# Differential-attention scores as fp32 products of 32 rows, four maps in four row quarters of the array, two heads at a time

## The chip, the cores and the metric

The kernel runs on one core of a Trainium2 chip. The metric is device time in microseconds of one execution, the median of several runs. The engines are TensorE (PE; its weight loads are listed as PEld), VectorE (DVE), ScalarE (ACT), GpSimd (POOL) and the DMA queues, which SyncE (SP), GpSimd and others issue to.

## The reference, cut to what matters

The program is a two-part transformer on 512 tokens of width 1024: a first block (mixing by two attentions, attention over a memory, a mixture of experts), then further layers. The change lies in the first step, differential attention with 8 heads, each with two maps of 32 features, and 64 value features:

```python
q1, q2 = q[..., :32], q[..., 32:]
k1, k2 = k[..., :32], k[..., 32:]
...
def attn_map(qb, kk):
    sc = jnp.einsum('bhqd,bhkd->bhqk', qb, kk, preferred_element_type=jnp.float32) * scale + bias
    return jax.nn.softmax(jnp.where(mask, sc, NEG_INF), axis=-1)
a = attn_map(qb1, k1) - lam * attn_map(qb2, k2)
o = jnp.einsum('bhqk,bhkd->bhqd', a.astype(v.dtype), v, preferred_element_type=jnp.float32)
o = o * lax.rsqrt(jnp.mean(o * o, axis=-1, keepdims=True) + RMS_EPS) * gain
```

The mask is causal and the bias is minus a head's slope times the distance of the positions, so a query block of 128 tokens needs 128, 256, 384 or 512 keys. A second attention (latent attention, 8 heads) follows, both results go through one output projection, and the residual is added.

## The kernel before

Activations are feature-major, `[128, 512]` per chunk. Large products are made of fp32r parts: an operand is split into a high part (ScalarE, L406 or L409) and a low part (VectorE, L407 or L410), and three products (L399, L400, L401, 24 of them to a block of 128 output features) replace one of fp32. Weights stream from DRAM through rings of buffers on SP's queue and are split in the same way.

The mixing stage (`mix`, L1719) works through the list `MSEQ` in this order, each letter a step: `p` queries and keys of a pair of heads, `v` values, `h` a head of differential attention, `r` the rotary table, `c`, `k`, `n` the projections and norms of latent attention, `m` keys and values of the memory. The list sets priorities; the tile framework orders the instructions of each engine when the program is built, so that steps interleave, and it sets the semaphores. An engine executes its own instructions in that order.

- `pair(c)` (L1756) makes queries and keys of heads 2c and 2c + 1. It evacuates a block's product times 1/rms (L1749, L1751) into a tile of the ring `sq` (three buffers), splits it into two more tiles of the same ring (L406, L407), writes the parts to DRAM, three times 32 rows for each map (L1766, tile `qkd`), and reads them back (L1771, tile `qk`) so that a map's 96 rows stand under each other. DMAs of this step are issued by GpSimd.
- `attend(h)` (L1857) then needs one fp32r product with 96 rows for a map's scores of a query block (L1872, tile `sc`, two banks). VectorE adds the distances and takes the minimum (L1874, L1878), ScalarE makes the exponentials and their sums (L1880), VectorE joins the two maps (L1884 to L1886). `av` transposes the result on TensorE (L2018, two banks), ScalarE copies it (L2020), and L2010 multiplies it with the values (`po`, two banks). At a head's end come square, sum, power on GpSimd (L1894) and scaling (L1895); after two heads the result is transposed (L1900) and split.

Latent attention uses the same six banks afterwards; its scores (L1969) are fp32 products with 128 rows. Elsewhere in the program, L728 and L1327 are fp32 scores with 64 rows; L1327 takes its two heads from rows 0 to 63 and 64 to 127 in turn. L1353 multiplies with the values, a head in each half of the array's columns. Two more banks (`pmm`) serve the projections everywhere.

Of the kernel before, what the change touches and what calls it, by code (L numbers as in the profile page):

```python
# [6 lines left out]
F32 = mybir.dt.float32  # L7
# [6 lines left out]
P = 128  # L14
# [13 lines left out]
MSEQ="v0 p1 h0 r0 v1 h1 p2 h2 c0 h3 c1 p3 h4 h5 k1 k0 n0 m0 h6 m1 h7 m2"  # L28
PQ=(0,4)
NB0=3  # L30
QP=6
# [13 lines left out]
SB3=7  # L45
# [12 lines left out]
# ---------------------------------------------------------------- host layout  # L58
# [50 lines left out]
def constants():  # L109
    """Arrays that depend on shapes alone, by the part that uses them."""  # L110
# [39 lines left out]
    # blocks of 8, and the blocks under and over the diagonal that a doubling joins  # L150
# [24 lines left out]
def pack(inp):  # L175
# [38 lines left out]
    # a piece holds the same input features for both experts of a pair  # L214
# [13 lines left out]
    # heads that share a block of features  # L228
# [47 lines left out]
# ---------------------------------------------------------------- kernel  # L276

class K:
    def __init__(self, tc, d, sm_off, phases=None, dbg=None):
        self.tc, self.nc, self.d = tc, tc.nc, d  # L280
        self.sm_off = sm_off
        self.dbg = dbg or {}
        self.phases = phases
        self.cst_off = {n: (ph,) + v for ph, c in constants().items() for n, v in c.off.items()}
        self.cst_t = {}
        self.nblk, self.gates = 3, []
        # pieces that the program starts with
        self.early = []
        self.lo_eng = None
# [4 lines left out]
    # -- small helpers  # L294
# [19 lines left out]
    def room(self, st, *, raw, parts):  # L314
        """Room for streamed weights: raw tiles, and tiles of each part; more of it until st closes."""
# [12 lines left out]
    def all_raw(self, st):  # L328
        """The room for parts is for raw tiles too, until st closes."""
# [9 lines left out]
    def experts(self):  # L339
        """The experts' weights in the order of their use."""  # L340
# [8 lines left out]
    def ahead(self):  # L349
        """Load one more piece of the experts' weights, behind the last load."""  # L350
# [7 lines left out]
    def piece(self, kind, dt):  # L358
        """The next tile of streamed weights, from the rings by turns."""
# [4 lines left out]
    def fetch(self, ap, kper):  # L364
        """Start the load of one streamed piece of kper chunks, in tiles of whole chunks."""
# [12 lines left out]
    def parts(self, raw):  # L378
        """A piece split into its two parts; the result gives both for chunk c, columns a to b."""
# [16 lines left out]
    def mm3(self, ps, a, b, first, last):  # L396
        """ps += (a0 + a1)^T (b0 + b1), without the product of the two low parts."""
# [14 lines left out]
    def rpow(self, out, sums, scale, tag="rp"):  # L412
        """out = (sums * scale + EPS) ** -0.5"""
# [6 lines left out]
    def stats(self, chunks, dim, tmp, ntok=T, bank=None, both=False):  # L420
        """Feature-major chunks -> 1/rms per token: token-major [P, nt] and broadcast [P, ntok]."""
# [24 lines left out]
    def rows_of(self, bc, rt, ps):  # L446
        """Token-major columns as rows that every partition has."""
# [7 lines left out]
    def two_norms(self, g1, g2, bank, pool):  # L455
        """Products' operand and factors for rms_norm(rms_norm(x) * g1) * g2; the first 1/rms as rows."""
# [5 lines left out]
        # sums of x^2 and of the squares of the first norm's results, side by side  # L462
# [26 lines left out]
    def norm_split(self, gname, pool=()):  # L489
        """Split x * gain into two parts; 1/rms is left for the products' results. GpSimd takes the chunks in pool."""  # L490
# [9 lines left out]
    def start(self, gname, both=False):  # L500
        """Split x * gain, and 1/rms."""
# [49 lines left out]
    def out_proj(self, src, hs):  # L551
        """x += W^T h."""
# [25 lines left out]
            # brings the functions' table in  # L578
# [44 lines left out]
    def last_norm(self, gname):  # L623
        """The result, rms_norm(x), by halves of the tokens."""
# [60 lines left out]
    def mem_keys(self, m, wk, n, dst):  # L685
        """Keys feature-major [P, n / 128, 256], kept in DRAM."""
# [9 lines left out]
    def mem_values(self, m, wv, n, dst):  # L696
        """Values [P, 2, n], kept in DRAM."""
# [7 lines left out]
    def mem_kv(self, src, pool, n):  # L705
        """Keys and values back on the chip."""
# [5 lines left out]
    def mem_attn(self, q, kv, dh, mh, ml, wk, ps_s, ps_t, ps_o, part=range(4)):  # L712
        """q: feature-major chunks times -1/sqrt(dh); mh, ml: [P, chunks, T] for the result."""
# [72 lines left out]
    # -- swiglu  # L786
    def ffn(self, l, mid=None, end=None):
        tc, nc, d = self.tc, self.nc, self.d
        hs, rt, bc = self.start(f"ln_ffn_2{l}")
        with ExitStack() as st:  # L790
# [6 lines left out]
            for half in range(2):  # L797
# [24 lines left out]
                # the very last by halves of the tokens, for the norm to start on  # L822
# [17 lines left out]
    def gdn(self):  # L840
        tc, nc, d = self.tc, self.nc, self.d
        with ExitStack() as st:
            e = lambda **k: st.enter_context(tc.tile_pool(**k))
            gp = e(name="gdp", bufs=1)
            # the first block's last norm and this one's in one; the residual waits in DRAM, its room is needed
# [22 lines left out]
            # gates  # L868
# [18 lines left out]
            def gates():  # L887
# [4 lines left out]
                # the other halves of what comes as 2 silu  # L892
# [29 lines left out]
                # gc as rows, exactly in three parts: a product spreads the sum of a head's over all partitions  # L922
# [29 lines left out]
            def silu2(y, t):  # L952
                """y = 2 silu(y); tanh is in the same table as exp."""
# [35 lines left out]
                # both come as 2 silu: 4 EPS  # L989
# [20 lines left out]
                # decays: column gc minus row gc  # L1010
# [12 lines left out]
                # its diagonal blocks of 8  # L1023
# [24 lines left out]
            def invert(h, A, Dg):  # L1048
                """Transposes of the inverses of a head's unit triangular matrices, by doubling the blocks.

                Chunks go by twos: of the second the transpose is inverted, so that at every doubling the two
                fill different rows and one product serves both. Chunks lie in the order 0, 2, 1, 3."""
                # heads by turns have their own room, so that two can be under way
# [9 lines left out]
                # blocks of 8 first, every row of an inverse on its lane, with its block's coefficients beside it  # L1063
# [29 lines left out]
                for lv in range(3, 7):  # L1093
# [4 lines left out]
                    def pick(t, odd):  # L1098
                        """Of every two blocks one of the first chunks, and the other of the second chunks."""
# [152 lines left out]
    def swa(self):  # L1252
# [3 lines left out]
        with ExitStack() as st:  # L1256
# [23 lines left out]
            # keys and values, with the gain on the weights  # L1280
# [27 lines left out]
            def attend(c, q):  # L1308
                """Heads c and c + 6."""
# [4 lines left out]
                for n0 in range(0, 4, 2):  # L1314
# [32 lines left out]
                    # a head in each half of the array's columns  # L1347
# [44 lines left out]
    # -- experts  # L1392
    def moe(self):
        tc, nc, d = self.tc, self.nc, self.d
        with ExitStack() as st:
# [13 lines left out]
            with ExitStack() as s2:  # L1409
# [3 lines left out]
                # 1/rms is left for the slots  # L1413
# [3 lines left out]
                # tokens on partitions  # L1417
# [31 lines left out]
                def first_max(p, n, pref, name):  # L1449
                    """One-hot of the first place of the maximum, and the maximum."""  # L1450
# [601 lines left out]
```

## Time and profile before

| | us |
|---|---|
| median of 3 runs | 2067.1 |
| lowest, highest | 2065.58, 2067.19 |
| span of the profiled execution | 2066.2 |
| TensorE busy in the span | 1970.3 |
| VectorE, ScalarE, GpSimd busy | 1041.0, 741.3, 378.4 |

The profile is of one execution, and its span runs from the first to the last instruction of the program; the median lies 0.9 us above it. Busy times are sums over the whole program, whose stages have different limits; matmuls are pipelined, so that a busy TensorE is not TensorE at its peak. The mixing stage takes roughly the first 300 us, and its differential attention the time up to about 222 us.

### The profile page before, as it was taken

What the parts mean: (1) busy time and instruction counts of PE and PEld (TensorE: products, weight loads), DVE (VectorE), ACT (ScalarE), POOL (GpSimd) and SP (SyncE); (2) the same over time, 40 slices, a digit from 0 to 9 for tenths busy, and PEclk for the clock granted to TensorE, in tenths of its full rate; (3) what the DMA queues carried; (4) which work ended last, traced back from release to release, by engine and by line L of the source; (5) the groups of instructions that cost most, each with busy time, mean ns of one, the idle gap of its engine ahead of it and who ended that gap; (6) DMA issues with size and microseconds to landing.
All of it is one profiled execution on the core that took longest, in us unless ns stands there. A gap on an engine that the chain in (4) does not pass through costs nothing.

```text
span 2066.2 us, 26427 instructions
## 1 busy us (share of the span) xinstructions
PE 1970.3 (95%) x10030; PEld 1520.2 (74%) x10030; DVE 1041.0 (50%) x2139; ACT 741.3 (36%) x1465; POOL 378.4 (18%) x364
## 2 busy tenths in 40 slices
PE   8689999989999999999999999999999999999997
PEld 6569668784555558778877788888876688888887
DVE  6368755661322236788855543343436654433434
ACT  4357653631111124344453332222325642222221
POOL 3223134110000001445412110011111021101111
PEclk9889999999999999999999999999999999999999
DMA  6754125149988962211112232332321033233322
GB/s 203 173 130 123 47 62 178 39 164 353 338 293 302 340 231 95 61 42 52 52 57 91 86 90 85 112 93 82 101 92 35 18 102 96 83 98 112 94 82 70
DMA packets 91458, 256.07 MB, mean 124 GB/s; under 512 B 18680, under 2 KB 21824, under 8 KB 91328
## 3 DMA queue, kind: packets, MB, share of 16 engines
q1 hardware_dynamic: 73520, 240.34, 35.0%
q0 software_dynamic: 16144, 12.66, 3.2%
q8 instruction: 81, 1.33, 0.3%
q10 hardware_dynamic: 1664, 1.34, 0.2%
q14 instruction: 49, 0.40, 0.1%
HBM read 241.65 MB, written 12.58 MB: 123 GB/s over the span
## 4 chain that ended last, share of the span: by engine, by line
PE 70%; DVE 4%; DMA 2%; ACT 1%; POOL 1%; issue 1%; DVEq 0%; ACTq 0%
PE mmp L399 16%; PE mmp L400 15%; PE mmp L401 15%; PE pgu L1548 6%; PE py L1548 3%; PE psx L1614 3%; PE pgt L1564 3%; DMA raw<-in_w_swa_dram 1%; PE sc L1327 1%; PE po L748 1%; DVE lo L407 1%; PE tp L961 1%; PE po L1353 1%; PE pt L1339 0%; DVE cv L949 0%
## 5 line engine op out<-in xcount | busy, mean ns | idle before, releaser
L399 PE MATMUL mmp<-xh,hi 128*128 128x512 f32 (+1 forms) x1328 | 523.4, 394 | 1.4 <-ACT xh L406 0.7
L400 PE MATMUL mmp<-xl,hi 128*128 128x512 f32 (+1 forms) x1328 | 517.5, 390 | 0.9 <-DVE xl L410 0.9
L401 PE MATMUL mmp<-xh,lo 128*128 128x512 f32 (+1 forms) x1328 | 517.0, 389 | 0.0
L406 ACT ACTIVATE hi<-raw 128x1024 fp32r<-128x1024 f32 (+2 forms) x256 | 252.4, 987 | 645.7 <-PE mmp L400 557.2
L407 DVE TENSOR_TENSOR lo<-raw,hi 128x1024 fp32r<-128x1024 f32 (+1 forms) x242 | 280.4, 1160 | 140.2 <-ACT hi L406 137.1
L399 PEld LDWEIGHTS mmp<-xh,hi 128*128 128x128 f32 x1328 | 253.3, 191 | 54.3 <-issue 3.0
L400 PEld LDWEIGHTS mmp<-xl,hi 128*128 128x128 f32 x1328 | 253.1, 191 | 50.5 <-issue 1.4
L401 PEld LDWEIGHTS mmp<-xh,lo 128*128 128x128 f32 x1328 | 252.8, 190 | 50.2 <-issue 0.7
L807 POOL TENSOR_TENSOR g<-g,rbc 128x512 f32<-128x512 f32 x44 | 75.5, 1716 | 509.0 <-ACT g L806 509.0
L400 PE MATMUL mmp<-alo,hi 128*128 128x512 f32 (+1 forms) x374 | 141.9, 380 | 0.0
L399 PE MATMUL mmp<-ahi,hi 128*128 128x512 f32 (+1 forms) x374 | 141.9, 380 | 0.0
L401 PE MATMUL mmp<-ahi,lo 128*128 128x512 f32 (+1 forms) x374 | 141.9, 379 | 0.0
L433 POOL TENSOR_TENSOR sqt<-sqt 128x512 f32<-128x512 f32 (+1 forms) x50 | 69.4, 1389 | 241.6 <-ACT sqt L429 223.7
L809 DVE TENSOR_TENSOR a<-mmp,g 128x512 f32<-128x512 f32 x44 | 30.4, 691 | 145.0 <-PE mmp L401 145.0
L805 DVE TENSOR_TENSOR g<-mmp,rbc 128x512 f32<-128x512 f32 x44 | 30.4, 691 | 112.5 <-PE mmp L401 112.5
L399 PEld LDWEIGHTS mmp<-ahi,hi 128*128 128x128 f32 x374 | 70.4, 188 | 14.1
L401 PEld LDWEIGHTS mmp<-ahi,lo 128*128 128x128 f32 x374 | 70.4, 188 | 14.1
L400 PEld LDWEIGHTS mmp<-alo,hi 128*128 128x128 f32 x374 | 70.4, 188 | 14.0
L1564 PEld LDWEIGHTS pgt<-G,tok 128*128 128x128 f32 x512 | 61.6, 188 | 10.9 <-issue 8.9
L943 POOL MEMSET pad<- 128x4 f32 x18 | 1.7, 102 | 368.3 <-DVE xl L410 346.8
L1564 PE MATMUL pgt<-G,tok 128*128 128x256 f32 x512 | 64.6, 282 | 1.0 <-ACT xl L1566 1.0
L1615 DVE TENSOR_TENSOR x<-psx,x 128x512 f32<-128x512 f32 x64 | 43.3, 687 | 43.2 <-PE psx L1614 42.3
(517 smaller groups left out, 3121.8 us busy)
## 6 DMA issues: line engine op xcount, KB each, us to landing
raw<-in_w_egu_dram SPq DMA_DIRECT2D x128, 512.0 KB, 7.9
raw<-in_w_gu_dram SPq DMA_DIRECT2D x88, 512.0 KB, 3.5
raw<-in_w_ed_dram SPq DMA_DIRECT2D x64, 512.0 KB, 8.1
raw<-in_w_out_dram SPq DMA_DIRECT2D x24, 512.0 KB, 3.6
raw<-in_w_gdn_dram SPq DMA_DIRECT2D x24, 512.0 KB, 3.6
raw<-in_w_dn_dram SPq DMA_DIRECT2D x32, 384.0 KB, 3.1
raw<-in_w_dn_dram SPq DMA_DIRECT2D x32, 320.0 KB, 2.8
raw<-in_w_qk_dram SPq DMA_DIRECT2D x12, 512.0 KB, 7.9
```

What stands on the lines that cost most here:

```text
L399: mm(ps, a[0], b[0], start=first, stop=False)
L400: mm(ps, a[0], b[1], start=False, stop=False)
L401: mm(ps, a[1], b[0], start=False, stop=last)
L406: nc.scalar.activation(hi, src, AF.Copy)
L407: (eng or nc.vector).tensor_tensor(lo, src, hi.bitcast(F32), OP.subtract)
L433: (nc.vector if i == len(chunks) - 1 else nc.gpsimd).tensor_tensor(acc, acc, s, OP.add)
L805: nc.vector.tensor_tensor(g, pg, bc, OP.mult)
L807: nc.gpsimd.tensor_tensor(g, g, bc, OP.mult)
L1548: nc.tensor.matmul(ps[hb], a[:, hb], w[b][:, o:o + 512], start=first, stop=last)
L1564: nc.tensor.matmul(pgt[:, 256 * j:256 * j + 256], toks[k][:, t, cs], G[:, t], start=k + t == 0, stop=k + t == 4)
L1614: nc.tensor.matmul(psx, ys[k][:, a, c * P:(c + 1) * P], ss[a], start=a + k == 0, stop=a + k == 2)
L1615: nc.vector.tensor_tensor(self.x[c], psx, self.x[c], OP.add)
```

## The change

Queries and keys of a pair of heads stay in two fp32 tiles of 128 rows: 32 rows for each of the four maps. `attend` takes a pair of heads, and a map's scores are one fp32 product of 32 rows at partition 0, 32, 64 or 96, each into a bank of its own. Splits, DRAM tile and DMAs of `pair` go. Differential attention gets a ring of five banks for scores and transposes and one bank for the output of a pair (both heads' steps at a pair's end are done at once); latent attention opens its own banks afterwards. The order list has four pairs in place of eight heads. Several rings change their size or place (queries and keys 4 tiles, softmax tiles 9 instead of 7, the split latent activations 3 tiles of their own), and comments are removed.

```diff
-MSEQ="v0 p1 h0 r0 v1 h1 p2 h2 c0 h3 c1 p3 h4 h5 k1 k0 n0 m0 h6 m1 h7 m2"
+MSEQ="v0 p1 v1 h0 r0 p2 c0 h1 c1 p3 h2 k1 k0 n0 m0 h3 m1 m2"
-QP=6
+QP=4
-SB3=7
+SB3=9
...
-            dp = e(name="mixd", bufs=2, space=bass.MemoryType.DRAM)
+            cq_p = e(name="mixc", bufs=3)
-            ps_s = e(name="ps_s", bufs=2, space=PSUM)
-            ps_t = e(name="ps_t", bufs=2, space=PSUM)
-            ps_o = e(name="ps_o", bufs=2, space=PSUM)
+            ps_d = dst.enter_context(tc.tile_pool(name="ps_d", bufs=5, space=PSUM))
+            ps_o = dst.enter_context(tc.tile_pool(name="ps_od", bufs=1, space=PSUM))
...
-                t = B("qk")
+                t = qp.tile([P, T], F32, name="qk", tag="qk")
...
             def pair(c):
-                dr = dp.tile([2, 4, 96, T], F32R, name="qkd", tag="qkd")
-                for x, slots in ((0, (0, 0, 1)), (1, (0, 1, 0))):
-                    t = qk(c + 4 * x)
-                    two = [self.sq.tile([P, T], F32R, name="qks", tag="sq") for k in range(2)]
-                    self.split(*two, t)
-                    for i, k in enumerate(slots):
-                        nc.gpsimd.dma_start(dr[x, :, 32 * i:32 * i + 32], two[k])
-                out = []
-                for a in range(2):
-                    out.append([D("qk")[:96] for x in range(2)])
-                    for x in range(2):
-                        nc.gpsimd.dma_start(out[a][x], dr[x, 2 * a:2 * a + 2].rearrange("m p t -> p m t"))
-                return out
+                return qk(c), qk(c + 4)
...
-            def attend(h):
+            def attend(c):
+                q, k = pairs[c]
+                slopes = [2.0 ** -(2 * c + a + 1) for a in range(2)]
+                po = ps_o.tile([P, 4, 2, 64], F32, name="po", tag="po")
...
                 for i in range(4):
                     n = (i + 1) * P
+                    sc = [ps_d.tile([P, T], F32, name="sc", tag="s")[:, :n] for m in range(4)]
+                    for m in range(4):
+                        r = slice(32 * m, 32 * m + 32)
+                        nc.tensor.matmul(sc[m], q[r, i * P:n], k[r, :n], start=True, stop=True)
                     es = []
-                    for m in range(2):
-                        ps = ps_s.tile([P, T], F32, name="sc", tag="sc")[:, :n]
-                        nc.tensor.matmul(ps, q[:, m, i * P:n], k[:, m, :n], start=True, stop=True)
+                    for m in range(4):
                         s = w3.tile([P, T], F32, name="s", tag="s")[:, :n]
-                        V.tensor_tensor_reduce(s, ps, dist[i], 1.0, 3e38, OP.add, OP.min,
-                                               mn[:, 2 * i + m:2 * i + m + 1])
+                        V.tensor_tensor_reduce(s, sc[m], dist[i], 1.0, 3e38, OP.add, OP.min,
+                                               mn[:, 4 * i + m:4 * i + m + 1])
...
+                    for a in range(2):
+                        for m in range(2):
+                            x = es[2 * a + m]
+                            nc.scalar.activation(x, x, AF.Exp, bias=mn[:, 4 * i + 2 * a + m:4 * i + 2 * a + m + 1],
+                                                 scale=-slopes[a], accum_out=sm[:, m, i, a:a + 1])
...
-                    self.av(es[0], i + 1, ps_t, wk, vd, po[:, i * 64:(i + 1) * 64], h)
+                        self.av(es[2 * a], i + 1, ps_d, wk, vd, po[:, i, a], 2 * c + a, "s")
...
-                if a:
-                    pt = ps_t.tile([P, 512], F32, name="pt", tag="pt")
-                    for i in range(4):
-                        nc.tensor.transpose(pt[:, i * P:(i + 1) * P], on[:, i], I)
-                    self.split(mixh[:, c], mixl[:, c], pt, gd)
+                pt = ps_d.tile([P, 512], F32, name="pt", tag="s")
+                for i in range(4):
+                    nc.tensor.transpose(pt[:, i * P:(i + 1) * P], on[:, i], I)
+                self.split(mixh[:, c], mixl[:, c], pt, gd)
...
+            dst.close()
+            ps_s = e(name="ps_s", bufs=2, space=PSUM)
+            ps_t = e(name="ps_t", bufs=2, space=PSUM)
+            ps_o = e(name="ps_o", bufs=2, space=PSUM)
...
-            oa = [t[:, k].bitcast(F32) for t in (D("oa"), D("oa")) for k in range(2)]
+            oa = [qp.tile([P, T], F32, name="oa", tag="qk") for c in range(4)]
```

The transposes of `av` and `turned` take the ring's tag as a new argument.

## Rows read from the trace of the kernel before

**Rows 1.** The page's second part: TensorE's busy tenths in 40 slices of 51.7 us.

```profile
PE   8689999989999999999999999999999999999997
```

**Rows 2.** Stretches: us; PE, PEld, DVE, ACT, POOL busy (x); PEclk; DMA share; GB/s.

```profile
60.00:150.00 90.00, 74.49 (x362) 62.73 (x363) 48.81 (x145) 38.12 (x89) 21.85 (x31) 0.86 0.70 159
150.00:180.00 30.00, 24.13 (x159) 22.46 (x158) 26.30 (x99) 23.04 (x69) 12.78 (x15) 0.83 0.43 109
180.00:222.00 42.00, 40.40 (x314) 37.39 (x312) 34.88 (x107) 30.04 (x76) 12.50 (x7) 1.00 0.36 120
sum 197.00, PE 166.27 PEld 147.38 DVE 127.10 ACT 101.75 POOL 56.38; mean PE 41.57 PEld 36.84 DVE 31.77 ACT 25.44 POOL 14.09
```

**Rows 3.** TensorE's waits, 25 to 230 us: total us, times, longest.

```profile
PE sc L1872 <- DVE mnd L1874: 11.7, 6, 6.3
PE mmp L399 <- DVE qk L1751: 11.2, 1, 11.2
...
PE sc L1872 <- issue: 2.5, 1, 2.5
```

**Rows 4.** VectorE in order of time: start, us, instruction, idle time before it.

```profile
61.88 0.69 DVE L407 TENSOR_TENSOR qks<-qk,qks 128x512 fp32r<-128x512 f32 x1 [11.69 <-DMA qkd<-qks]
...
104.77 0.69 DVE L407 TENSOR_TENSOR qks<-qk,qks 128x512 fp32r<-128x512 f32 x1 [9.08 <-DMA qkd<-qks]
...
137.42 0.69 DVE L407 TENSOR_TENSOR qks<-qk,qks 128x512 fp32r<-128x512 f32 x1 [3.91 <-DMA qkd<-qks]
```

**Rows 5.** DMA issues to 230 us: count, KB each, median us to landing.

```profile
qkd<-qks POOLq DMA_DIRECT2D x24, 256.0 KB, 9.5
qk<-qkd POOLq DMA_DIRECT2D x16, 384.0 KB, 6.4
```

**Rows 6.** TensorE's groups by form, 222 to 300 us: busy us, mean ns, idle.

```profile
L1969 PE MATMUL sc<-km,qm 128*128 128x512 f32 x16 | 8.0, 593 | 0.0
...
L1969 PE MATMUL sc<-km,qm 128*128 128x256 f32 x16 | 4.8, 380 | 0.0
```

**Rows 7.** TensorE in order of time around fp32 scores with 64 rows.

```profile
1036.53 0.39 PE L401 MATMUL mmp<-xh,lo 128*128 128x512 f32 x1
1036.85 0.70 PE L728 MATMUL sc<-memkv,mq 64*128 64x256 f32 x2
1037.48 0.38 PE L1113 MATMUL pz<-Y,Tm 128*128 128x128 f32 x1
...
1594.45 0.51 PE L400 MATMUL mmp<-xl,hi 128*128 128x512 f32 x1
...
1596.68 0.70 PE L1327 MATMUL sc<-kT,q 64*128 64x256 f32 x4
1597.31 0.33 PE L1353 MATMUL po<-pT,vv 128*64 128x128 f32 x2
```

**Rows 8.** TensorE in order of time: values v1, the first and some later scores.

```profile
49.12 0.38 PE L399 MATMUL mmp<-hi,xh 128*128 128x256 f32 x1
...
70.10 0.41 PE L1872 MATMUL sc<-qk 96*128 96x128 f32 x2 [2.52 <-issue]
...
139.56 0.78 PE L1872 MATMUL sc<-qk 96*128 96x128 f32 x2 [2.33 <-DVE mnd L1874]
...
198.66 0.48 PE L1872 MATMUL sc<-qk 96*128 96x512 f32 x1
198.98 0.28 PE L400 MATMUL mmp<-lo,xh 128*128 128x256 f32 x1
199.10 0.39 PE L1872 MATMUL sc<-qk 96*128 96x512 f32 x1
199.33 0.28 PE L401 MATMUL mmp<-hi,xl 128*128 128x256 f32 x1
```

**Rows 9.** Groups by line, 25 to 222 us: busy us, mean ns, idle and its releasers.

```profile
L407 DVE TENSOR_TENSOR qks<-qk,qks 128x512 fp32r<-128x512 f32 x8 | 5.5, 690 | 33.1 <-DMA qkd<-qks 32.4 <-ACT qks L406 0.7
...
L1894 POOL TENSOR_TENSOR rrd<-rsd,mhalf 128x4 f32<-128x4 f32 x7 | 8.9, 1270 | 32.2 <-DVE rsd L1893 30.1 <-DVE rp L417 1.4 <-DVE mnd L1878 0.7
```

More of the change, by code (lines that the diff above doesn't have):

```diff
@@ L1742, in mix @@
             Y = lambda name, n: self.tiny.tile([P, n], F32, name=name, tag=name)
+            dst = st.enter_context(ExitStack())
+            ps_d = dst.enter_context(tc.tile_pool(name="ps_d", bufs=5, space=PSUM))
+            ps_o = dst.enter_context(tc.tile_pool(name="ps_od", bufs=1, space=PSUM))
             def qk(j):
-                ps = self.proj(d["w_qk"], j, hs, bank=ps_o.tile([P, T], F32, name="po", tag="po") if j in PQ else None)
-                t = B("qk")
+                ps = self.proj(d["w_qk"], j, hs, bank=ps_d.tile([P, T], F32, name="po", tag="s") if j in PQ else None)
+                t = qp.tile([P, T], F32, name="qk", tag="qk")
                 if j < 4:
@@ L1816, in mix @@
             mixh, mixl = self.half()
-            pairs, cq, kms, cqs, mem, ons = {0: nxt}, [], [], [], [], {}
+            pairs, cq, kms, cqs, mem = {0: nxt}, [], [], [], []
             def latent_q(j):
@@ L1855, in latent_norms @@
                 return mq, rkv, bkv, (t[:, 0], t[:, 1])
-            def attend(h):
-                c, a = divmod(h, 2)
-                if a == 0:
-                    ons[c] = wk.tile([P, 4, P], F32, name="on", tag="on", bufs=1)
-                on = ons[c]
-                q, k = pairs[c][a]
-                slope = 2.0 ** -(h + 1)
-                po = ps_o.tile([P, 512], F32, name="po", tag="po")[:, :256]
-                mn, sm = Y("mnd", 8), Y("smd", 8)
+            def attend(c):
+                q, k = pairs[c]
+                slopes = [2.0 ** -(2 * c + a + 1) for a in range(2)]
+                po = ps_o.tile([P, 4, 2, 64], F32, name="po", tag="po")
+                mn, sm = Y("mnd", 16), Y("smd", 16)
+                sm = sm.rearrange("p (m i a) -> p m i a", m=2, a=2)
@@ L1878, in attend @@
-                    V.tensor_scalar(mi, mi, slope, None, op0=OP.mult)
-                    for m in range(2):
-                        nc.scalar.activation(es[m], es[m], AF.Exp, bias=mi[:, m:m + 1], scale=-slope,
-                                             accum_out=sm[:, 4 * m + i:4 * m + i + 1])
-                    s0, s1 = (sm[:, 4 * m + i:4 * m + i + 1] for m in range(2))
-                    V.reciprocal(s1, s1)
-                    V.scalar_tensor_tensor(s1, s0, nlam, s1, op0=OP.mult, op1=OP.mult)
@@ L1886, in attend @@
-                    V.scalar_tensor_tensor(es[0], es[1], s1, es[0], op0=OP.mult, op1=OP.add)
-                    self.av(es[0], i + 1, ps_t, wk, vd, po[:, i * 64:(i + 1) * 64], h)
-                sq = wk.tile([P, 256], F32, name="osq", tag="osq", bufs=1)
-                nc.scalar.activation(sq, po, AF.Square)
-                rs, rr = Y("rsd", 4), Y("rrd", 4)
-                V.tensor_reduce(rs, sq.rearrange("p (a b) -> p a b", a=4), AX, OP.add)
-                V.scalar_tensor_tensor(rr, sm[:, 0:4], EPS, sm[:, 0:4], op0=OP.mult, op1=OP.mult)
@@ new lines, in attend @@
+                    for a in range(2):
[3 more added lines that the diff above has]
+                                                 scale=-slopes[a], accum_out=sm[:, m, i, a:a + 1])
+                        s0, s1 = (sm[:, m, i, a:a + 1] for m in range(2))
+                        V.reciprocal(s1, s1)
+                        V.scalar_tensor_tensor(s1, s0, nlam, s1, op0=OP.mult, op1=OP.mult)
+                        V.scalar_tensor_tensor(es[2 * a], es[2 * a + 1], s1, es[2 * a], op0=OP.mult, op1=OP.add)
+                        self.av(es[2 * a], i + 1, ps_d, wk, vd, po[:, i, a], 2 * c + a, "s")
@@ new lines, in attend @@
+                pf = po.rearrange("p i a b -> p (i a) b")
+                sq = wk.tile([P, 8, 64], F32, name="osq", tag="osq", bufs=1)
+                nc.scalar.activation(sq, pf, AF.Square)
+                rs, rr = Y("rsd", 8), Y("rrd", 8)
+                V.tensor_reduce(rs, sq, AX, OP.add)
+                s0 = sm[:, 0].rearrange("p i a -> p (i a)")
+                V.scalar_tensor_tensor(rr, s0, EPS, s0, op0=OP.mult, op1=OP.mult)
+                V.scalar_tensor_tensor(rs, rs, 1.0 / 64, rr, op0=OP.mult, op1=OP.add)
@@ new lines, in attend @@
+                nc.gpsimd.tensor_tensor(rr, rs, self.mhalf[:, 0:8], OP.pow)
+                on = wk.tile([P, 4, P], F32, name="on", tag="on", bufs=1)
+                V.tensor_tensor(on.rearrange("p i (a b) -> p (i a) b", a=2), pf,
+                                rr.unsqueeze(2).to_broadcast([P, 8, 64]), OP.mult)
+                pt = ps_d.tile([P, 512], F32, name="pt", tag="s")
+                for i in range(4):
+                    nc.tensor.transpose(pt[:, i * P:(i + 1) * P], on[:, i], I)
@@ L2011, in av, with turned @@
                                   start=k == 0, stop=k == nk - 1)
-    def turned(self, p, nk, ps_t, wk):
+    def turned(self, p, nk, ps_t, wk, tag="pt"):
         nc = self.nc
-        pt = ps_t.tile([P, 512], F32, name="pt", tag="pt")
+        pt = ps_t.tile([P, 512], F32, name="pt", tag=tag)
         for k in range(nk):
```

13 lines of the change are left out of this document (6 added, 7 removed).

## The prediction

> **What bounds the kernel now.** I read the page first. TensorE is busy for 9 tenths or more of nearly every slice, so what it waits for is what can be won; of the forty slices the first three (to 155 us) are the thin ones, at 8, 6 and 8 tenths [rows 1]. That is the mixing stage, where the changed code runs. Everything behind it takes its results, so a microsecond won there is won at the end, unless a later stage waits for something else.
>
> The table of stretches then sizes the loss [rows 2]. From 25 to 222 us TensorE is busy for 166.3 of 197 us, so 30.7 us are idle. Its clock averages 0.86 from 60 to 150 us and 0.83 from 150 to 180, which costs up to 0.14 x 74.5 + 0.17 x 24.1 = 10.4 + 4.1 = 14.5 us more (the averages count idle time too, so this is the upper end).
>
> TensorE's waits name the places [rows 3]. One of 11.2 us ends with VectorE's evacuation in L1751. Another, of 6.3 us, ends with L1874. A third, 2.5 us before the first score, has no releaser in the profile. VectorE's order of time shows what lies behind the named ones [rows 4]: just before L1751 it sat 11.69 us in the split L407 until the write to DRAM (`qkd<-qks`) had landed, and at 104.77 it sat 9.08 us for the same reason, with the scores' evacuations queued behind it. The split's two results live in a ring of three buffers that is free only when the write has landed, and such a write takes 9.5 us, the read back 6.4 [rows 5]. So the stall is a transfer's latency, met by engines that execute in order. A wait of that kind at 137.42, 3.91 us on VectorE, comes just ahead of 2.3 us of TensorE's at 139.56 [rows 8]. Sum on TensorE: 11.2 + 6.3 + 2.5 + 2.3 = 22.3 us.
>
> **What the change removes.** The 24 writes and 16 reads go, with their issue on GpSimd's queue, and so do eight splits on ScalarE and VectorE (5.5 us on the latter) [rows 5, 9]. None of this busy time is on the path by itself. The waits are: 22.3 us, and the half-clock stretches behind them. I take 8 of the 10.4 us from 60 to 150. Together **-30 us**. Bounds: -22 if the clock would fall anyway, -36 if the rest of the stage's small waits go too.
>
> **What it adds on TensorE.** Before, a score is one product of stacked fp32r rows. The latent attention shows what fp32 costs: L1969 makes eight products of each width (four pairs of two heads) and has 16 instructions of each, so a product is two; 512 columns take 593 ns and 256 take 380, or 0.83 ns per column for each instruction, 1.67 per product [rows 6]. An fp32r product of 512 columns, undisturbed, starts 0.23 us before the next, 0.45 ns per column [rows 8]. All 16 maps have 128 + 256 + 384 + 512 = 1,280 columns each, 20,480 in all. Before, they cost 0.23 to 0.32 us per 512 columns, 9 to 13 us; I take 11. After, one behind the other they would stream for 20,480 x 1.67 ns = 34 us, and four at a time for 8.5.
>
> No row shows quarters, but halves of the rows are shown: L1327 puts its heads into rows 0 to 63 and 64 to 127, and four of its instructions of 256 columns (two products) leave the next start 0.63 us away, just as two instructions (one product) of L728 of the same size do [rows 7]. So products in different rows do run side by side, when they stand next to each other in the queue.
>
> The same rows give the price of going in and out of this mode. From L401's start to the one behind L728 it is 0.95 us; less 0.23 of its own and 0.43 of L728's stream, 0.30 is left, and a full-size product behind L1327 lasts 0.51 instead of L401's 0.39 us. So 0.3 to 0.42 us a visit; I take 0.4. A map alone then costs 2.13 + 4 x 0.4 = 3.73 us, 16 of them 60 us. In fours it is 15, in twos 30. The Trainium skill, "TensorEngine Tiling (Array Packing)", under Key Properties, says that a change of tiling mode drains the engine; the trace agrees with 0.3 to 0.42 us. The skill's "TensorE: Matmul & The Clock Gate", Part 3, measured 3.07 times for four row tiles instead of four; by it the fours' stream would be 34 / 3.07 = 11 instead of 8.5 us, an estimate that adds 2.6 us.
>
> How often do they stand together? The first step of a pair of heads finds four free banks, so its four go together. After that five banks are shared by four scores and the transposes, and each bank comes back when VectorE has read it. In the trace of before, scores mostly stand alone between projections for this reason [rows 8]. On the other hand an fp32 score holds TensorE longer, so that more banks are free when it is done. I take twos on average: 30 - 11 = **+19 us**, with +4 (fours) and +49 (all alone) as the ends.
>
> **What it moves.** Heads go in pairs, and the first pair stands behind the value projection v1 instead of in front of it. That costs nothing: v1 starts at 49.12, ahead of the first score at 70.10 already [rows 8]. Without the round trip the first scores can follow v1 at about 60. The loads of the projections stay on SP's queue in the order of use, and no step passes a GpSimd transfer any more. From 150 to 180 us VectorE is busy for 26.3 of 30 us, and TensorE idles 5.9 us and loses up to 4.1 by the clock [rows 2], since attention that came late is bunched there. Spread from 60 us on, I take **-4 us** of these 10, with 0 and -8 as bounds.
>
> The output bank of a pair is now single. The next pair's products with the values wait for square, sum, power and scaling (GpSimd's power alone is 1.27 us [rows 9]), some 3 us, three times. The projections between the pairs cover that; without them it is +9. The other edits (rings, the latent results in another ring, a new set of banks between the attentions) add no instruction; the latent projections that need no such bank cover the change of banks. If they did not, the wait would be that of one head's end, about 3 us.
>
> **Sum.** -30 + 19 - 4 = -15 us, against a span of 2066.2; the median of the runs is 2067.1, 0.9 above it. So 2052.
>
> **The rivals.**
> - *Fours.* The banks come back fast enough and most scores go in fours: -30 + 4 - 8 = -34, 2033 us. For it speaks that the four are issued in a row; against it, that five banks serve six users.
> - *Scores alone (slower).* The mechanism is the visit's price, 0.4 us and a stream that overlaps with nothing. It decides where the scores cost 30 + 4 + 11 = 45 us, which is 60 / 45 = 1.3 products per visit. At 1.2 it is 50 - 11 - 30 = +9, 2076 us; all alone, +19, 2086. The lone scores of before [rows 8] speak for it.
> - *The change doesn't do what it says.* Quarters, unlike halves, run one after the other: 34 us of stream and 16 to 32 visits give 40 to 47 us, -30 + 29 to 36 - 4 = -5 to +2, about 2066. Against it speaks the overlap of the halves.
> - *VectorE and its chain become the bound.* Behind 60 us it needs 48.8 + 26.3 + 34.9 - 4 (six of the eight splits) = 106 us [rows 2, 9]. At its best rate, 34.9 of 42 us, that ends at 188 and binds nothing. If waits inside a pair keep it at 0.66, it ends at 220, where the stage ends now: 2065.
>
> **How the numbers follow.** Twos, 2042 to 2062 us: 0.42. Fours, 2028 to 2042: 0.20. Quarters in a row: 0.08; VectorE's chain: 0.12, both about 2060 to 2070. Scores alone, above 2071: 0.18. The prediction is the likeliest, 2052. Leaving out a tail of about 0.1 on either side gives 2030 to 2076. About 0.2% (4 us) is what a measurement of this kernel can tell from no change. Faster by more: 0.42 + 0.20 + 0.08 of the middle cases = 0.70; within: 0.12; slower: 0.18.
>
> **What would show it.** Right: no idle time that a transfer ends between 25 and 222 us; the clock near 1.00 from 60 to 150 us; first scores at about 60 us; instructions of the score line, 128 of them, in runs of four (two products) a few nanoseconds apart; the latent attention starting some 15 us before 218. Wrong: runs of two with about 0.3 us around them everywhere; score instructions of one step that start a full stream apart; TensorE waiting for L1874's results in every step; or a new wait at the output bank. A wait for weights from 60 us on would make the whole sum wrong, since it leaves the projections out as cover.

## The result and the profile after

The changed kernel takes 2115.4 us (median of 4, 2113.1 to 2121.1), the kernel before 2067.1 beside it: a ratio of 1.0231, 95% interval 1.0213 to 1.0250. It is slower by 48 us, where 2052 was predicted and 2030 to 2076 given as the range. The profiled execution took 2121.1 us with a span of 2118.9.

The page's second part, TensorE's busy tenths and its granted clock in 40 slices of 53 us, shows where. The loss is in the first five or six slices, the stage that was changed; behind it both kernels look alike [rows 1].

```profile
PE   5988799989999999999999899999999999999997
...
PEclk9877799999999998999999999999999999999999
```

The table of stretches cuts that stage into three (us; PE, PEld, DVE, ACT, POOL busy (x); granted clock; DMA share; GB/s). In the kernel before, TensorE was busy for 15.70 of the first 25 us and for 51.30 of the 65 behind them.

```profile
0.00:25.00 25.00, 1.78 (x9) 1.79 (x9) 18.82 (x17) 13.02 (x18) 11.19 (x12) 1.00 0.67 244
25.00:90.00 65.00, 65.00 (x379) 56.66 (x378) 27.47 (x64) 23.98 (x46) 3.30 (x5) 1.00 0.28 90
90.00:274.00 184.00, 152.32 (x774) 116.59 (x775) 97.97 (x294) 80.28 (x196) 24.91 (x18) 0.76 0.18 54
```

So TensorE starts 14 us poorer, then works without a gap for 65 us, as the prediction wanted, and from 90 us on is idle for 32 of 184 us at three quarters of its clock. (The record of the clock begins at 30.9 us here and at 16.2 us before; what lies ahead of it is printed as 1.00. It was half clock: up to 30.9 us products of 256 columns start 0.21 us apart, as they do at a recorded 0.50 in e4_again at 167 us, and behind it 0.12.) The first latent score, at 218.3 us before, comes at 273.5: 55 us later. Summed over windows of 2 us from 26 us to that score, busy time times what the clock lacked is 33.3 us after and 12.6 before; idle time is 31.7 and 30.6. The 55 us are therefore about 14 (start), 21 (clock), 1 (idle) and 20 of additional work. The same count from 0, with half clock ahead of the records, gives 15 idle, 21 clock and 19 work. Of the 55, 45 are left when the stage's last results are added, and 53 at the end of the span.

TensorE's waits name the two places (us in total, times, longest).

```profile
PE stp L437 <- DVE sqt L433: 23.2, 1, 23.2
PE pt L2014 <- DVE s L1876: 15.4, 11, 3.6
PE po L2006 <- ACT pT L2016: 6.8, 6, 1.7
PE pt L2014 <- DVE mnd L1866: 3.2, 1, 3.2
```

The first is the start: TensorE's first instruction of all is the sum of the norm, at 23.2 us. The others stand in place of the waits of before [rows 3], which have gone. TensorE in order of time, in the second pair of heads, shows how they arise (start, us, instruction, idle time before it and what ended it).

```profile
134.47 0.71 PE L1857 MATMUL sc<-qk 32*128 32x256 f32 x6
135.10 0.43 PE L2006 MATMUL po<-vd,pT 128*128 128x64 f32 x2
135.47 0.69 PE L1857 MATMUL sc<-qk 32*128 32x256 f32 x2
136.09 0.43 PE L2006 MATMUL po<-vd,pT 128*128 128x64 f32 x2
138.78 0.69 PE L2014 MATMUL pt<-cst_all,s 128*128 128x128 f32 x2 [2.25 <-DVE s L1876]
139.77 0.69 PE L2014 MATMUL pt<-cst_all,s 128*128 128x128 f32 x2 [0.29 <-DVE s L1876]
140.39 1.65 PE L1857 MATMUL sc<-qk 32*128 32x384 f32 x6
141.97 1.11 PE L2006 MATMUL po<-vd,pT 128*128 128x64 f32 x4
143.02 1.64 PE L1857 MATMUL sc<-qk 32*128 32x384 f32 x2
```

Read it as a circle. A step's scores (x6 is three products, the fourth comes behind) go out, VectorE and ScalarE make probabilities of them, the transposes L2014 wait for the last result of that (L1876), and only behind the transposes stand the next step's scores. VectorE meanwhile waits for TensorE, at 142.07 for 2.35 us:

```profile
142.07 0.56 DVE L1861 CUSTOM_DVE_ANT_0 s<-sc,dist 128x384 f32<-128x384 f32 x1 [2.35 <-PE sc L1857]
```

Each engine waits for the other by turns. The four maps themselves do what the change says: the six instructions of 134.47 last 0.71 us together, hardly more than the two of 135.47 alone (0.69), so the quarters overlap.

### The profile page after: what moved, and what is told of

Its sections match the earlier page's. It is cut to its first block, busy times and chain, and to the rows that moved or that the text cites. A ratio compares the mean times of both kernels' runs of the same rounds, so it can differ in the third digit from the quotient of the medians.

```text
span 2118.9 us, 26396 instructions
## 1 busy us (share of the span) xinstructions
PE 2008.4 (95%) x10094; PEld 1539.6 (73%) x10094; DVE 1036.4 (49%) x2115; ACT 739.9 (35%) x1453; POOL 343.6 (16%) x320
## 4 chain that ended last, share of the span: by engine, by line
PE 70%; DVE 3%; ACT 1%; POOL 1%; DMA 1%; issue 0%; DVEq 0%; ACTq 0%
PE mmp L399 16%; PE mmp L400 16%; PE mmp L401 15%; PE pgu L1548 6%; PE psx L1614 3%; PE py L1548 3%; PE pgt L1564 3%; PE sc L1327 1%; PE po L748 1%; PE tp L961 1%; PE po L1353 1%; PE sc L728 1%; PE pt L1339 0%; DVE cv L949 0%; POOL sqt L433 0%; PE pg L968 0%
## 5 line engine op out<-in xcount | busy, mean ns | idle before, releaser
L1548 PE MATMUL pgu<-raw,xh 128*64 128x512 f32 x256 | 61.4, 611 | 3.3 <-PEq L1644 3.3
```

The lines of the kernel that those rows point to most:

```text
L1548: nc.tensor.matmul(ps[hb], a[:, hb], w[b][:, o:o + 512], start=first, stop=last)
```

## The experiments

The theory after this reading was that two things done to PSUM cost the time, and not the scores. *Start:* with `PQ=(0,4)` the first query projection takes its bank from `ps_d`, whose first bank lies where the norm's sums lie; it must wait for them. *Ring:* scores and transposes draw on one ring of five banks. If a ring hands out its banks in the order of the requests, then four scores, two transposes and four scores again are ten requests to five banks, and a round begins on banks that the round before still holds. No row shows which bank a tile lies in; the experiments move the banks and look at the waits. The rival: the fp32 scores' own time on TensorE, with its drains, is what costs, and the idle time only follows from it.

| kernel | us | ratio to before, 95% | latent scores, first start and last end |
|---|---|---|---|
| before | 2067.1 | 1 | 218.3, 280.1 |
| after | 2115.4 | 1.0231 (1.0213 to 1.0250) | 273.5, 325.3 |
| e1_bank | 2099.5 | 1.0144 (1.0121 to 1.0167) | 258.0, 309.8 |
| e2_ownpt | 2100.1 | 1.0144 (1.0125 to 1.0163) | 225.6, 309.9 |
| e3_both | 2077.6 | 1.0033 (1.0015 to 1.0051) | 231.4, 283.2 |
| e4_heads | 2062.0 | 0.9974 (0.9955 to 0.9993) | 210.5, 267.9 |
| e5_banks321 | 2063.0 | 0.9968 (0.9954 to 0.9983) | 219.0, 275.9 |
| e6_fp32r | 2049.1 | 0.9891 (0.9872 to 0.9909) | 202.4, 259.8 |
| e4_again | 2058.1 | 0.9942 (0.9924 to 0.9960) | 217.1, 274.5 |
| e7_norms_last | 2061.6 | 0.9958 (0.9942 to 0.9974) | 220.9, 272.7 |
| e8_heads_norms_last | 2070.4 | 0.9998 (0.9986 to 1.0010) | 224.5, 282.2 |

The kernel before ran beside each group of kernels, at 2068.3 us for e1 to e4, 2070.2 for e5, e6 and e4_again, 2070.8 for e7 and e8; so ratios are compared, not times. After had 2067.1 beside it; by the ratios the gains of e1, e2 and e3 over it, given in times below, are 18, 18 and 41 us. All kernels but after lie within 2% of before, so that what is said of them rests on the intervals.

**e1_bank: the start alone.** The output's pool is made first, so that `ps_d` no longer begins on the norm's bank.

```diff
-            ps_d = dst.enter_context(tc.tile_pool(name="ps_d", bufs=5, space=PSUM))
             ps_o = dst.enter_context(tc.tile_pool(name="ps_od", bufs=1, space=PSUM))
+            ps_d = dst.enter_context(tc.tile_pool(name="ps_d", bufs=5, space=PSUM))
```

> The changed kernel with the output bank of a pair allocated ahead of the five shared banks, so that the first projection no longer starts in the bank that the sums of the norm hold. Theory (two causes: a late start of TensorE, and attention steps in series on the shared banks): TensorE starts near 7 us instead of 23 us and the time falls by 11 to 16 us, to about 2102. Rival (the attention alone sets the end of the stage, the late start is covered): less than 4 us gained, 2112 to 2115. Rival (fp32 scores are what costs): the same 11 to 16 us, and the attention stays as long as it is.

Measured: 2099.5, 15.8 us less. TensorE begins with the projection, when its weights are split:

```profile
7.67 0.80 PE L399 MATMUL po<-xh,hi 128*128 128x512 f32 x1 [7.67 <-ACT hi L406]
```

Two lines of allocation in another order, and not one instruction more or less, are worth 16 us. The waits of the ring stay (13.9 us for L1876).

**e2_ownpt: the ring alone.** Transposes get a bank of their own, scores keep four; the late start stays.

```diff
-            ps_d = dst.enter_context(tc.tile_pool(name="ps_d", bufs=5, space=PSUM))
+            ps_d = dst.enter_context(tc.tile_pool(name="ps_d", bufs=4, space=PSUM))
+            ps_t = dst.enter_context(tc.tile_pool(name="ps_td", bufs=1, space=PSUM))
...
-                        self.av(es[2 * a], i + 1, ps_d, wk, vd, po[:, i, a], 2 * c + a, "s")
+                        self.av(es[2 * a], i + 1, ps_t, wk, vd, po[:, i, a], 2 * c + a)
```

> The changed kernel with four banks for the scores and one of their own for the transposes, in place of five shared ones; the late start stays. Theory (steps in series): the scores of the next step are issued while this one is still in its softmax, the waits of transposes on VectorE's L1876 shrink from 15 us to a few, the clock between 90 and 280 us rises, and 25 to 40 us are gained: 2075 to 2090. Rival (the price of fp32 scores on TensorE): the same products at the same price, 2110 to 2115. Rival (the order list has used up the projections as filler): less than 10 us gained.

Measured: 2100.1, 15.2 us less, which is under what was expected. The waits for L1876, 15.4 us in after, are gone. The stretches show why it is not more:

```profile
25.00:150.00 125.00, 124.12 (x692) 99.50 (x691) 79.38 (x226) 61.18 (x145) 7.41 (x9) 1.00 0.23 72
150.00:180.00 30.00, 28.22 (x102) 21.01 (x100) 15.65 (x45) 11.37 (x27) 5.09 (x6) 0.51 0.16 53
180.00:222.00 42.00, 42.00 (x262) 33.77 (x261) 25.92 (x66) 18.55 (x45) 10.08 (x5) 0.94 0.37 120
222.00:250.00 28.00, 17.02 (x72) 12.83 (x70) 6.84 (x20) 8.85 (x22) 1.64 (x1) 0.57 0.00 1
```

To 150 us the circle is gone: TensorE is busy for 124.12 of 125 us, at full clock from 31 us on. From 150 to 180 the clock is at half, of which e5 tells more. From 222 to 250 TensorE is idle again, for a reason that e3 shows better.

**e3_both: both edits.** Output, transposes and scores have 1 + 1 + 4 banks, in this order.

> Both: output bank ahead, and a bank of its own for the transposes. Theory: the two gains add up, 2050 to 2070, at or a little below the kernel before. Rival (fp32 scores cost what was lost): 2100, no better than the first alone. Rival (list): 2090 to 2100.

Measured: 2077.6, 37.8 us less than after (the two alone add to 31), but 0.3% above before still. Most of the rest is in one place, the last pair of heads, in order of time:

```profile
202.13 1.11 PE L1893 MATMUL pt<-cst_all,on 128*128 128x128 f32 x4 [5.30 <-DVE on L1889]
204.81 0.47 PE L2015 MATMUL pt<-cst_all,s 128*128 128x128 f32 x1 [1.56 <-DVE xl L410]
205.65 0.69 PE L2007 MATMUL po<-vd,pT 128*128 128x64 f32 x2 [0.37 <-ACT pT L2017]
206.13 0.42 PE L2015 MATMUL pt<-cst_all,s 128*128 128x128 f32 x1
206.92 0.69 PE L2007 MATMUL po<-vd,pT 128*128 128x64 f32 x2 [0.37 <-ACT pT L2017]
```

All scores are out by 193.6 us, and no projection stands in TensorE's order from 191 to 224 us, but the transposing bank is a ring of one: the third pair's results (L1893) must pass it before the last pair's probabilities may enter, and then each transpose waits for the copy of the one before. TensorE is idle for 11.6 of the 42 us from 180 to 222, at a mean clock of 0.73.

**e5_banks321: two transposing banks, three for scores,** otherwise e3.

> The rest of the loss, tested on the third experiment's kernel (output, transposes and scores each with banks of their own, 1 + 1 + 4): the banks are dealt 3 for scores, 2 for transposes, 1 for output. Theory: behind 180 us the last pair of heads went through one transposing bank with no projection left between, 12 us of idle TensorE and a clock of 0.5 behind it; with two banks the steps of one pair overlap, projections are left for the last pair, and the time falls 5 to 12 us under that kernel, to 2062 to 2072. Rival (visits): with three score banks the fourth map of every step stands alone, 16 more visits of 0.4 us and a stream that overlaps nothing, 10 us or more, so 2080 or above and a score occupancy above 35 us instead of 27.

Measured: 2063.0, a ratio of 0.9968 against e3's 1.0033, so 13 us less. The rival did not come: the scores stand in 36 visits (runs of score instructions with nothing between) instead of 34, not in 16 more. They hold TensorE 32.9 us instead of 27.4, each instruction counted from its start to the next one's without idle time, but much of that is the clock: weighted with it, it is 28.1 instead of 27.0. Between after and e5 only banks are dealt in another way: the change as such isn't slower. From 26 us to the first latent score TensorE is idle for 2.3 us.

What e5 loses is clock, and without idling:

```profile
142.00:150.00 8.00, 7.05 (x30) 3.90 (x28) 7.77 (x22) 7.44 (x21) 2.08 (x3) 0.89 0.01 3
150.00:180.00 30.00, 30.00 (x123) 23.26 (x122) 18.52 (x65) 14.11 (x42) 6.35 (x8) 0.50 0.16 53
```

At 0.50 (1.2 of 2.4 GHz) for 30 us, with no idle time, up to 15 us are lost. Ahead of that, TensorE did this:

```profile
142.67 0.50 PE L437 MATMUL stp<-ones,sqt 128*128 128x1 f32 x4
143.10 1.13 PE L1858 MATMUL sc<-qk 32*128 32x512 f32 x4
144.16 0.38 PE L437 MATMUL stp<-ones,sqt 128*128 128x1 f32 x2
144.47 1.12 PE L1858 MATMUL sc<-qk 32*128 32x512 f32 x2
145.52 0.38 PE L437 MATMUL stp<-ones,sqt 128*128 128x1 f32 x2
145.77 0.63 PE L1893 MATMUL pt<-cst_all,on 128*128 128x128 f32 x4
146.24 0.27 PE L2015 MATMUL pt<-cst_all,s 128*128 128x128 f32 x1
147.37 2.19 PE L1858 MATMUL sc<-qk 32*128 32x512 f32 x4 [0.86 <-DVE mnd L1862]
```

No projection stands among them. If the clock fell once, from 1.00 to 0.50, the mean of 0.89 from 142 to 150 us puts the fall at 148.2, within the last of these rows.

**e7_norms_last: is it this gathering?** The latent norms (`n0`, which makes the sums L437) go from the middle of e5's list to its end; `h3` also comes ahead of `m0`.

```diff
-MSEQ="v0 p1 v1 h0 r0 p2 c0 h1 c1 p3 h2 k1 k0 n0 m0 h3 m1 m2"
+MSEQ="v0 p1 v1 h0 r0 p2 c0 h1 c1 p3 h2 k1 k0 h3 m0 m1 m2 n0"
```

> The kernel of the fifth experiment (banks 3 + 2 + 1) with one step of the list moved: the latent norms, n0, go from the middle of the list to its end. In the fifth experiment TensorE ran at half clock from 149 to 184 us though it was never idle there; that fall came at the end of some 8 us (142.7 to 150) in which the norms' sums, 32-row scores, transposes and products of 64 columns stood together with no projection between, and it cost about 17 us. Theory: it is this gathering of narrow products that loses the clock; spread among the projections the clock stays at 1.00 in the middle of the stage, and the time falls from 2063 by 7 to 15 us, to 2048 to 2056. Rival: the clock falls all the same, or the norms at the end are a chain that nothing covers in front of the latent attention, 6 us or more; then 2060 to 2070.

Measured: 2061.6; the intervals of e5 and e7 overlap, so the time is the same. The same two stretches, with the ones ahead of and behind them:

```profile
25.00:142.00 117.00, 117.00 (x629) 88.10 (x629) 73.72 (x221) 58.72 (x143) 10.18 (x12) 0.97 0.24 77
142.00:150.00 8.00, 8.00 (x43) 5.19 (x42) 7.12 (x24) 5.73 (x15) 0.70 (x1) 1.00 0.39 131
150.00:180.00 30.00, 30.00 (x221) 25.33 (x219) 22.59 (x72) 17.27 (x45) 3.25 (x2) 1.00 0.29 97
180.00:222.00 42.00, 36.24 (x221) 31.17 (x221) 20.21 (x46) 20.33 (x41) 16.07 (x9) 0.88 0.22 65
```

The clock held where the norms had been, as the theory had it: from 26 us to the first latent score it costs 7.7 us instead of 18.8. The rival was right about the end: from 190 us on nothing covers the norms, TensorE waits 2.8 us for their squares and 2.0 for the last pair, and the clock falls there instead. Idle time up to the first latent score rises from 2.3 to 5.8 us. Clock and idle time together are 7.6 us less than in e5, but that score comes 1.9 us later, partly because 21 more projection products (some 4.5 us) stand ahead of it. The last latent score ends 3.2 us earlier, and 1.1 us of that are left in the span. Where the rest went was not traced.

The theory is not shown either. The 0.97 in the first stretch is a fall from 115.9 to 122.7 us, and there projections did stand between the scores, without idle time:

```profile
112.56 0.47 PE L399 MATMUL mmp<-xh,hi 128*128 128x512 f32 x1
112.97 1.12 PE L1858 MATMUL sc<-qk 32*128 32x512 f32 x2
114.02 0.50 PE L400 MATMUL mmp<-xl,hi 128*128 128x512 f32 x1
114.45 1.12 PE L1858 MATMUL sc<-qk 32*128 32x512 f32 x2
115.50 0.50 PE L401 MATMUL mmp<-xh,lo 128*128 128x512 f32 x1
115.84 0.58 PE L399 MATMUL mmp<-xh,hi 128*128 128x512 f32 x1
116.22 0.63 PE L400 MATMUL mmp<-xl,hi 128*128 128x512 f32 x1
```

A fall of 3.4 us in e5, at 76.5 us, has like surroundings.

**e4_heads: the prediction's terms by themselves.** The kernel before, with its list, its single heads and its 2 + 2 + 2 banks; only the stacking through DRAM goes, and the scores are fp32 from row quarters. Two rings change with it, as in the change (queries and keys 4 tiles, the split latent activations 3 of their own). The line of the product:

```diff
-                        nc.tensor.matmul(ps, q[:, m, i * P:n], k[:, m, :n], start=True, stop=True)
+                        r = slice(64 * a + 32 * m, 64 * a + 32 * m + 32)
+                        nc.tensor.matmul(ps, q[r, i * P:n], k[r, :n], start=True, stop=True)
```

> The kernel before with one part of the change alone: queries and keys stay in fp32 tiles, no split, no DRAM round trip, scores as fp32 products of 32 rows; heads one at a time, the list and the two-two-two banks as before. Theory: what the prediction said of the round trip holds (30 us of waits and half clock go) and fp32 scores in twos cost some 19: 2045 to 2060. Rival (fp32 scores cost more than the round trip): slower than before, 2070 to 2090. Rival (the round trip was hidden): 2067 to 2085.

> The fourth experiment's kernel unchanged, for a closer number beside the two others of this call: 2057 to 2066.

Measured: 2062.0, and 2058.1 in the second group, ratios of 0.9974 and 0.9942: faster by 5 and 12 us, with intervals that overlap by a little. From 26 us to the first latent score TensorE idles 1.4 us in both profiles, where the kernel before idled 30.6; the scores hold it, counted as in e5, for 34.6 and 35.8 us instead of 15.3. The two profiled spans, 2055.7 and 2061.7, differ mainly by how long the clock stayed down behind 145 us, for about 10 us or 24 (5.1 and 12.0 us lost). The second one:

```profile
25.00:138.00 113.00, 112.51 (x626) 87.56 (x627) 73.93 (x216) 55.46 (x134) 7.23 (x8) 1.00 0.26 80
138.00:150.00 12.00, 11.47 (x60) 8.68 (x59) 10.75 (x37) 8.30 (x24) 3.96 (x4) 0.80 0.00 0
150.00:168.00 18.00, 18.00 (x73) 14.20 (x73) 10.92 (x36) 9.86 (x28) 5.92 (x8) 0.50 0.27 89
```

**e6_fp32r: the price of fp32.** e4 with queries and keys as fp32r, one instruction for each score instead of two.

```diff
-                t = qp.tile([P, T], F32, name="qk", tag="qk")
+                t = qp.tile([P, T], F32R, name="qk", tag="qk")
```

> The price of the fp32 scores, tested on the fourth experiment's kernel (the list, head by head order and banks of before, without the round trip through DRAM). Queries and keys are rounded to fp32r, so that a score is one instruction instead of two: that gives up the low part of both and is no longer the computation in full precision. Theory: TensorE is never idle in that stage, so what its scores hold less is won; they held 35.5 us against 18.7 before, and the time falls by 12 to 20 us, to 2042 to 2050. Rival: VectorE and ScalarE's chain (evacuations, exponentials) sets the stage's length by now, and TensorE's saving turns into idle time: 2056 or above.

Measured: 2049.1, a ratio of 0.9891 against e4_again's 0.9942, so 10.5 us less: of the theory's sign, and a little under its 12 to 20. The scores hold TensorE for 18.0 us instead of 35.8, counted as in e5; the 35.5 and 18.7 of the expectation had some idle time in them. The groups by line, 20 to 230 us, of e4_again and of e6 (busy time there includes overlap with the neighbours):

```profile
L1859 PE MATMUL sc<-qk 32*128 32x128 f32 (+3 forms) x128 | 38.6, 513 | 0.6 <-DVE mnd L1861 0.5
```

```profile
L1859 PE MATMUL sc<-qk 32*128 32x128 f32 (+3 forms) x64 | 20.5, 427 | 0.7 <-DVE mnd L1861 0.7
```

Of the 17.8 us won on TensorE, 14.7 reach the first latent score and 10.3 the end of the span. Up to that score the clock costs 8.5 us instead of 12.0, and TensorE idles 4.9 us instead of 1.4, so the chain over VectorE and ScalarE begins to show.

**e8_heads_norms_last.** e4 with `n0` last and `c1`, a projection of latent attention, moved from ahead of `p3` to behind `h4`, so that the last pair's queries and keys come one step earlier.

> The kernel of the fourth experiment (scores in fp32 head by head, the banks of before, no round trip through DRAM) with the same move of n0 to the end of the list, and the last key and query pair one head earlier. That kernel was at half clock from 146 us on for 11 us in one profile and for 22 in another. Theory: without that stretch 5 to 10 us less than its 2058 to 2062, 2050 to 2056, the lowest of these kernels in full fp32 or split precision. Rival: as for the other kernel of this call, 2058 or above.

Measured: 2070.4, as slow as before, and slower than e4_again (its interval and that of the first e4 touch). The rival holds: TensorE is idle for 3.8 of the 18 us from 204 to 222, where the norms stand bare, and a new gap at 138 to 144 (4.3 of 6 us busy) brings the clock down in another place. Two things were moved at once, so their shares aren't known.

## Why the prediction was wrong

**The step that failed** is "The first step of a pair of heads finds four free banks, so its four go together. After that five banks are shared by four scores and the transposes, and each bank comes back when VectorE has read it." From this I worked out how many products stand together, and nothing else. That count was not even bad: after has 26 visits for its 64 products, 2.5 in each, better than the twos I took. What I left out is that the shared ring is an order. The next scores stand behind this step's transposes, these behind VectorE's and ScalarE's whole chain; the projections between were issued long before. Waits of this kind stood in the sum at nothing. Waits and half clock were to fall by 34 us; up to the first latent score they rose by 22 (idle time 1, clock 21). Giving transposes banks of their own takes that away (e2 and e3, 15 and 22 us; e5, 13 more): from e1's ratio of 1.0144 to e5's 0.9968 it is 36 us, and the idle time up to the first latent score goes from 32.8 us in e1 to 14.7 in e3 and 2.3 in e5.

**A second step failed with it**, "The other edits (rings, the latent results in another ring, a new set of banks between the attentions) add no instruction". They add none and cost 16 us (e1), where the change of banks was put at 3 us at most. By the program a pool made first begins on the bank that the norm's sums still hold, and the first projection of the whole kernel went into it; e1's order of two lines confirms it by its effect.

**-30 us for the round trip** was right where nothing else took its place. In after, from 25 to 90 us, no idle time is left and the clock, from 30.9 us on, is 1.00; the first score comes at 51.0 us. Behind 90 us the waits of the ring use all of it up. e4 shows the full amount: 29.2 us less idle time, and 7.5 or 0.6 less lost to the clock, over the whole stage.

**+19 us for the scores** came out in e4, +19.3 and +20.5 by the time that scores hold TensorE, but partly by luck. Both terms were too low, 11 for 15.3 and 30 for 34.6 or 35.8, and the second is made of two errors that offset each other in part: 42 visits instead of the 32 assumed, at a lower price. After's own scores, in 26 visits, hold TensorE for 26.8 us, only 11.5 more than before's. On the price: in e5's rows at 144.47 a lone product of 512 columns holds TensorE for 1.05 us, two together at 143.10 for 1.06; less 0.85 of stream that leaves 0.2, where I took 0.4 with 0.3 as the lower bound. The Trainium skill, "TensorEngine Tiling (Array Packing)", Key Properties, has the change of mode drain the engine; these rows agree that there is a price and put it at 0.2 us behind the scores.

**-4 us for less bunching** is not shown. From 150 to 180 us before loses up to 10 to idling and clock together [rows 2]. The first profile of e4 loses 2.7 there (busy for 30.00 at a mean clock of 0.91), the second 9.6 (0.68), e5 up to 15, e7 nothing: it hangs on when the clock falls and how long it stays down. Together with the -30 it is -34, where e4 shows -36.7 and -29.8. I had taken half clock as something that waits cause, so that it would go with them.

**The single output bank** shows no wait in e5, whose idle time is 2.3 us in all; in e3 the wait at L1893 shows what it would be without cover, 5.3 us once, though there the single transposing bank has a part in it.

**The rivals.** None of the four happened as it was priced. The slower one had the right sign and the wrong mechanism: its +9 to +19 over before needs scores that cost 39 to 49 us more than before's, and after's hold TensorE only 11.5 us longer. The nearest was VectorE's chain, which names waits inside a pair: it put VectorE's rate at 0.66 at worst and the time at 2065, and from 60 us to the first latent score VectorE is busy for 109.4 of 213.5 us, a rate of 0.51. "TensorE waiting for L1874's results in every step" stood among what would make the prediction wrong, and is close to what the profile shows (transposes that wait for L1876, further down the same chain), but it had no price and no chance.

**What stays open.** The additional work up to the first latent score in after, 19 us with every instruction's hold weighted with the clock, is 4.6 of scores, 5.0 of products with the values, 4.7 of transposes and 4.8 of projections. A part is moved ahead of that score: 24 projection products, 20 with the values and 7 transposes (the latent attention itself lasts 51.8 us instead of 61.8). Why the remaining transposes and products with the values hold TensorE longer was not traced. Why the clock stayed down for 10 us in one profile of e4 and 24 in another isn't settled either.

## What to carry to other kernels

A ring of banks is an order as well as a number: when one ring serves two steps of a chain, the later step's request can hold up the next round's first. So count, for each ring, what stands between two requests, and give producer and consumer rings of their own even if each is smaller. And when pools move, ask what held that memory before: an edit that adds no instruction can still make the first one wait.

## What the runs showed of the hardware

- Products in different quarters of the rows overlap almost wholly: six fp32 instructions (three products) of 256 columns at 134.47 us last 0.71 us and two last 0.69. The trace has the starts of such instructions 6 to 7 ns apart.
- TensorE's clock can fall without idle time. In e7 it was at 0.50 from 115.9 to 122.7 us though TensorE was busy for 117.00 of the 117 us from 25 to 142, and projections stood between lone scores of 32 rows. In e5 it went from 1.00 to 0.50 at about 148 us, with 0.95 us of idle time behind 142 us, behind norm sums of one column, scores of 32 rows and transposes with no projection between; in e7 it stayed at 1.00 in that place. No run here separates what does it. The Trainium skill, "TensorE: Matmul & The Clock Gate", A second HAM failure mode: psum-queue depth-cycling, tells of another kernel in which short idle times between groups of products that cycle through PSUM banks make the clock go down and up. After agrees (its clock falls at 136.8 us, behind idle times of 0.80 and 0.44 us at 133 and 134); the fall in e7 has no idle time ahead of it.
- At half clock a busy TensorE shows no idle time: 30 us of e5 at 0.50, busy for 30.00, are worth up to 15. Busy time has to be read together with the granted clock.
